# A row softmax on one core: sixteen equal loads become ten loads of 3, 5, 8 and 16 rows per partition, with a store plan of their own

## The chip, the cores and the metric

One core of a Trainium2 chip. The time is device microseconds of one launch. The kernel before was run four times: 162.23 to 162.66 us, median 162.4 us. The profile shown here is of an execution of 162.53 us.

## The reference

```python
def reference(x):                       # x: 16 x 1024 x 512, float32
    x_max = np.max(x, axis=-1, keepdims=True)
    exp_x = np.exp(x - x_max)
    return (exp_x / np.sum(exp_x, axis=-1, keepdims=True)).astype(np.float32)
```

It is a softmax over the last axis. There are 16384 rows of 512 values. Input and output are 33.55 MB each, and nothing but these crosses between HBM and the core's SBUF.

## The kernel before

The 16384 rows are cut into 16 chunks (`CHUNKS`), each of 1024 rows: 8 rows for every one of the 128 partitions. In HBM the 8 rows of one partition lie side by side, so that a load or a store moves 128 runs of 16 KB, 2 MB together. SBUF holds 12 such chunks (`SLOTS`), 96 rows or 192 KB of every partition.

Each chunk passes through five functions.

- `load` (L68) is one DMA on SP's queue, from HBM into one of the 12 buffers.
- `rowmax` (L73) is one VectorE reduction over the 8 rows, which gives 128x8 negated maxima (`shift`).
- `exps` (L79) is 8 ScalarE activations, one for each row: the exponential with the maximum as its bias, written in place, with the sum of the row beside it (`sums`).
- `scale` (L91, L93) is one VectorE reciprocal of the 8 sums and 8 VectorE multiplications in place, one for each row.
- `store` (L100) is one DMA on ScalarE's own queue, from SBUF to HBM. A wait of this DMA stands in ScalarE's order of work, so that the activations of later chunks are held up behind it.

The order on each engine is that in which the program writes it (`manual_schedule`): load, rowmax and exps of chunk k, then scale and store of chunk k-1. VectorE therefore does the maximum of chunk k while the exponentials of chunk k-1 are made, and then scales chunk k-1. Loads 12 to 15 use the buffers of chunks 0 to 3 and wait for the stores of those to land. The DMAs share eight completion semaphores in turn, and a DMA waits for the one that had its semaphore before: load 6, for example, waits until load 0 has landed. Some waits of loads and of stores come from that alone.

`first_load_at_the_head` puts the first load ahead of the barrier with which the program opens.

Of the kernel before, what the change touches and what calls it, by code (L numbers as in the profile page):

```python
# [1 line left out]

# [4 lines left out]

F32 = mybir.dt.float32
EXP = mybir.ActivationFunctionType.Exp
AX = mybir.AxisListType.X  # L10


CHUNKS = [8] * 16

SLOTS = {8: 12}


def first_load_at_the_head(nc):

    main, body = nc.main_func.blocks[0], nc.main_func.blocks[1]  # L20
    dmas = [i for i in body.instructions if type(i).__name__ == "InstDMACopy"]
    load = dmas[0]
    assert load.engine == mybir.EngineType.SP
    body.instructions.remove(load)
    barrier = next(
        n
        for n, i in enumerate(main.instructions)
        if i.engine == mybir.EngineType.SP and type(i).__name__ == "InstDrain"
    )
    main.instructions.insert(barrier, load)  # L30


@with_exitstack
def kernel(
    ctx: ExitStack,
    tc: tile.TileContext,
    x: bass.AP,
    out: bass.AP,
):
    nc = tc.nc  # L40
    nc.at_finalize(first_load_at_the_head)
    P = nc.NUM_PARTITIONS

    x_flat = x.flatten_outer_dims()
    out_flat = out.flatten_outer_dims()
    n, d = x_flat.shape
    assert n == P * sum(CHUNKS)


    src, dst, at = [], [], 0  # L50
    for R in CHUNKS:
        for flat, views in ((x_flat, src), (out_flat, dst)):
            part = flat[at : at + P * R, :]
            views.append(part.rearrange("(p r) d -> p r d", r=R))
        at += P * R

    data = ctx.enter_context(tc.tile_pool(name="data", bufs=1))
    stats = ctx.enter_context(tc.tile_pool(name="stats", bufs=4))

    K = len(CHUNKS)  # L60
    tiles = [None] * K
    shift = [None] * K
    sums = [None] * K

    def load(k):
        R = CHUNKS[k]
        tiles[k] = data.tile([P, R, d], F32, name=f"x{R}", tag=f"x{R}", bufs=SLOTS[R])
        nc.sync.dma_start(out=tiles[k], in_=src[k])  # L68

    def rowmax(k):  # L70
        R = CHUNKS[k]
        shift[k] = stats.tile([P, R], F32, name=f"shift{R}", tag=f"shift{R}")
        nc.vector.reduce_max(out=shift[k], in_=tiles[k], axis=AX, negate=True)  # L73

    def exps(k):
        R = CHUNKS[k]
        sums[k] = stats.tile([P, R], F32, name=f"sums{R}", tag=f"sums{R}")
        for r in range(R):
            nc.scalar.activation(  # L79
                out=tiles[k][:, r, :],  # L80
                in_=tiles[k][:, r, :],
                func=EXP,
                bias=shift[k][:, r : r + 1],
                scale=1.0,
                accum_out=sums[k][:, r : r + 1],
            )

    def scale(k):
        R = CHUNKS[k]
        recip = stats.tile([P, R], F32, name=f"recip{R}", tag=f"recip{R}")  # L90
        nc.vector.reciprocal(out=recip, in_=sums[k])  # L91
        for r in range(R):
            nc.vector.tensor_scalar_mul(  # L93
                out=tiles[k][:, r, :],
                in0=tiles[k][:, r, :],
                scalar1=recip[:, r : r + 1],
            )

    def store(k):
        nc.scalar.dma_start(out=dst[k], in_=tiles[k])  # L100

    with tc.manual_schedule():
        for k in range(K):
            load(k)
            rowmax(k)
            exps(k)
            if k >= 1:
                scale(k - 1)
                store(k - 1)
        scale(K - 1)  # L110
        store(K - 1)


# [1 line left out]
_INS = ['x']  # L115
_OUTS = [((16, 1024, 512), 'float32')]


# [23 lines left out]
```

## Time and profile before

| | |
|---|---|
| time, median of 4 runs | 162.4 us |
| the profiled execution | 162.53 us, its span 160.7 us |
| VectorE (DVE) busy | 123.8 us, 77% of the span |
| ScalarE (ACT) busy | 93.2 us, 58% |
| bytes moved by DMA | 67.14 MB, mean 418 GB/s |
| first load | issued at 0.00 us, landed by 7.85 us |
| last store | issued at 149.08 us |

The span runs from the first instruction of the program to its last; 1.8 us of the execution's time lie around it. "GB/s" in the slices counts every byte once, whether it is read from HBM or written to it. In the queue table, q1 is SP's queue (the loads), q10 is ScalarE's (the stores).

### The profile page before, as it was taken

To read this page: it belongs to the slowest core of one execution; us is meant where nothing else is said; L and a number is where in the kernel's file an instruction comes from. 1 tells how busy PE (TensorE), PEld (TensorE's weight loads), DVE (VectorE), ACT (ScalarE), POOL (GpSimd) and SP (SyncE) were. 2 spreads that over 40 slices of the span, in tenths; PEclk is the share of its full clock that TensorE was granted. 3 is DMA by queue.
4 is the path that set the end of the run, shared out by engine and by line. 5 is a ranking of instruction groups with operands and counts; after the bars stand their busy time and mean duration, and the time that the engine had idled before them with its cause. 6 is when DMAs were issued, how large, how long until landed. Compare 5 with 4: busy or idle time off the path is not lost.

```text
span 160.7 us, 527 instructions
## 1 busy us (share of the span) xinstructions
DVE 123.8 (77%) x160; ACT 93.2 (58%) x257; POOL 0.2 (0%) x4
## 2 busy tenths in 40 slices
DVE  0098799999999999985960089999999999967000
ACT  0029985868677685076002987859595959592000
POOL 0000000000000000000000000000000000000000
DMA  7999999999999999999999999999999999999994
GB/s 241 412 448 424 428 453 338 424 430 428 424 444 436 418 424 436 440 428 424 444 428 428 428 424 448 424 426 428 424 453 424 428 424 432 444 424 428 440 428 175
DMA packets 4611, 67.14 MB, mean 418 GB/s; under 512 B 512, under 2 KB 512, under 8 KB 512
## 3 DMA queue, kind: packets, MB, share of 16 engines
q1 hardware_dynamic: 2304, 33.56, 49.9%
q10 hardware_dynamic: 2304, 33.56, 48.8%
q14 instruction: 3, 0.02, 0.0%
HBM read 33.55 MB, written 33.55 MB: 417 GB/s over the span
## 4 chain that ended last, share of the span: by engine, by line
DMA 52%; DVE 31%; ACT 7%; SPq 1%; issue 1%; ACTq 0%; DVEq 0%
DMA x<-in_x_dram 52%; DVE shift L73 16%; DVE x L93 14%; ACT x L79 7%; SPq L68 1%; DVE recip L91 1%; ACTq L100 0%; DVEq L137 0%; ACTq L79 0%
## 5 line engine op out<-in xcount | busy, mean ns | idle before, releaser
L79 ACT ACTIVATE x<-x,shift 128x512 f32<-128x512 f32 x128 | 90.5, 708 | 44.5 <-DVE shift L73 21.1
L73 DVE TENSOR_REDUCE shift<-x 128x8 f32<-128x4096 f32 x16 | 70.6, 4414 | 9.1 <-DMA x<-in_x_dram 9.1
L93 DVE TENSOR_SCALAR x<-x,recip 128x512 f32<-128x512 f32 x128 | 52.1, 481 | 0.6
L79 ACT ACTIVATION_READ_ACCUMULATOR x<-x,shift 128x1 f32 x128 | 23.9, 187 | 0.0
L91 DVE RECIPROCAL recip<-sums 128x8 f32<-128x8 f32 x16 | 3.1, 195 | 15.6 <-ACT x L79 15.6
L79 ACT ACT_TABLE_LOAD x1 | 1.3, 1283 | 7.9 <-DMA x<-in_x_dram 7.9
L126 POOL MEMSET const-uint8-127<- 128x1 uint8 x1 | 0.1, 103 | 0.0
L126 POOL MEMSET const-bfloat16-1.0<- 128x1 bf16 x1 | 0.1, 102 | 0.0
L126 POOL MEMSET const-float32-0.0<- 128x1 f32 x1 | 0.1, 99 | 0.2 <-issue 0.2
L126 POOL MEMSET const-float32-1.0<- 128x1 f32 x1 | 0.1, 99 | 0.0
## 6 DMA issues: line engine op xcount, KB each, us to landing
x<-in_x_dram SPq DMA_DIRECT2D x16, 2048.0 KB, 42.5
out_dram<-x ACTq DMA_DIRECT2D x16, 2048.0 KB, 17.7
```

The source lines that it names most:

```text
L68: nc.sync.dma_start(out=tiles[k], in_=src[k])
L73: nc.vector.reduce_max(out=shift[k], in_=tiles[k], axis=AX, negate=True)
L79: nc.scalar.activation(out=tiles[k][:, r, :], in_=tiles[k][:, r, :], func=EXP, bias=shift[k][:, r : r + 1], scale=1.0, accum_out=sums[k][: ...
L91: nc.vector.reciprocal(out=recip, in_=sums[k])
L93: nc.vector.tensor_scalar_mul(out=tiles[k][:, r, :], in0=tiles[k][:, r, :], scalar1=recip[:, r : r + 1],)
L126: nc = _bacc.Bacc("TRN2", target_bir_lowering=False, num_devices=1)
```

## The change

The 12 buffers become one array of 96 rows per partition, `held`, and every chunk has a fixed place in it (`CHUNKS` holds pairs of row count and first row). There are ten chunks, of 3, 5, 8 and seven times 16 rows. Eight loads (96 rows) are issued ahead of everything; load 8 goes where chunks 0, 1 and 2 were and is issued once the last of their stores is written, and load 9 goes where chunk 3 was.

A chunk of 16 rows is worked on in two groups of 8 rows, so that `rowmax`, `exps` and `scale` keep their size but for the first two chunks (3 and 5 rows). `FINISH_BEFORE` has VectorE scale chunks 0, 1 and 2 before it begins on the next chunk, instead of after that chunk's maximum. From chunk 3 on the order is as before.

A store covers 3, 5 and 8 rows for the first three chunks, 8 rows for each half of chunks 3, 4 and 5 (`STORE_ROWS`), and 16 rows for chunks 6 to 9. `ON_ACT` is empty, so all loads stay on SP's queue, and `AT_HEAD` puts one load ahead of the barrier, as before. A partition's rows within a chunk still lie side by side in HBM, so a load of 16 rows moves 128 runs of 32 KB; a store of half a chunk moves 128 runs of 16 KB that stand 32 KB apart.

```diff
@@ -10,24 +10,43 @@
 AX = mybir.AxisListType.X
 
 
-CHUNKS = [8] * 16
+CHUNKS = [
+    (3, 0), (5, 3), (8, 8), (16, 16), (16, 32), (16, 48), (16, 64), (16, 80), (16, 0), (16, 16),
+]
+SBUF_ROWS = 96
 
-SLOTS = {8: 12}
+EARLY = 8
+AFTER_STORE = {2: [8], 3: [9]}
+
+GROUP = 8
+
+FINISH_BEFORE = (1, 2, 3)
+
+STORE_ROWS = {3: 8, 4: 8, 5: 8}
+
+ON_ACT = ()
+
+AT_HEAD = {mybir.EngineType.SP: 1}
 
 
-def first_load_at_the_head(nc):
+
+def loads_at_the_head(nc):
 
     main, body = nc.main_func.blocks[0], nc.main_func.blocks[1]
-    dmas = [i for i in body.instructions if type(i).__name__ == "InstDMACopy"]
-    load = dmas[0]
-    assert load.engine == mybir.EngineType.SP
-    body.instructions.remove(load)
-    barrier = next(
-        n
-        for n, i in enumerate(main.instructions)
-        if i.engine == mybir.EngineType.SP and type(i).__name__ == "InstDrain"
-    )
-    main.instructions.insert(barrier, load)
+    for engine, count in AT_HEAD.items():
+        loads = [
+            i
+            for i in body.instructions
+            if i.engine == engine and type(i).__name__ == "InstDMACopy"
+        ][:count]
+        barrier = next(
+            n
+            for n, i in enumerate(main.instructions)
+            if i.engine == engine and type(i).__name__ == "InstDrain"
+        )
+        for load in loads:
+            body.instructions.remove(load)
+        main.instructions[barrier:barrier] = loads
 
 
 @with_exitstack
@@ -38,17 +57,17 @@
     out: bass.AP,
 ):
     nc = tc.nc
-    nc.at_finalize(first_load_at_the_head)
+    nc.at_finalize(loads_at_the_head)
     P = nc.NUM_PARTITIONS
 
     x_flat = x.flatten_outer_dims()
     out_flat = out.flatten_outer_dims()
     n, d = x_flat.shape
-    assert n == P * sum(CHUNKS)
+    assert n == P * sum(R for R, _ in CHUNKS)
 
 
     src, dst, at = [], [], 0
-    for R in CHUNKS:
+    for R, _ in CHUNKS:
         for flat, views in ((x_flat, src), (out_flat, dst)):
             part = flat[at : at + P * R, :]
             views.append(part.rearrange("(p r) d -> p r d", r=R))
@@ -56,59 +75,78 @@
 
     data = ctx.enter_context(tc.tile_pool(name="data", bufs=1))
     stats = ctx.enter_context(tc.tile_pool(name="stats", bufs=4))
+    held = data.tile([P, SBUF_ROWS, d], F32, name="held")
+    place = [held[:, s : s + R, :] for R, s in CHUNKS]
 
-    K = len(CHUNKS)
-    tiles = [None] * K
-    shift = [None] * K
-    sums = [None] * K
+
+    groups = []
+    for k, (R, _) in enumerate(CHUNKS):
+        m = max(1, round(R / GROUP))
+        cuts = [R * i // m for i in range(m + 1)]
+        since = 0
+        for a, b in zip(cuts, cuts[1:]):
+            ends = b == R or b - since >= STORE_ROWS.get(k, R)
+            groups.append((k, a, b, since if ends else None))
+            since = b if ends else since
+    shift = [None] * len(groups)
+    sums = [None] * len(groups)
 
     def load(k):
-        R = CHUNKS[k]
-        tiles[k] = data.tile([P, R, d], F32, name=f"x{R}", tag=f"x{R}", bufs=SLOTS[R])
-        nc.sync.dma_start(out=tiles[k], in_=src[k])
+        queue = nc.scalar if k in ON_ACT else nc.sync
+        queue.dma_start(out=place[k], in_=src[k])
 
-    def rowmax(k):
-        R = CHUNKS[k]
-        shift[k] = stats.tile([P, R], F32, name=f"shift{R}", tag=f"shift{R}")
-        nc.vector.reduce_max(out=shift[k], in_=tiles[k], axis=AX, negate=True)
+    def rowmax(g):
+        k, a, b, _ = groups[g]
+        shift[g] = stats.tile([P, b - a], F32, name="shift", tag="shift")
+        nc.vector.reduce_max(
+            out=shift[g], in_=place[k][:, a:b, :], axis=AX, negate=True
+        )
 
-    def exps(k):
-        R = CHUNKS[k]
-        sums[k] = stats.tile([P, R], F32, name=f"sums{R}", tag=f"sums{R}")
-        for r in range(R):
+    def exps(g):
+        k, a, b, _ = groups[g]
+        sums[g] = stats.tile([P, b - a], F32, name="sums", tag="sums")
+        for r in range(a, b):
             nc.scalar.activation(
-                out=tiles[k][:, r, :],
-                in_=tiles[k][:, r, :],
+                out=place[k][:, r, :],
+                in_=place[k][:, r, :],
                 func=EXP,
-                bias=shift[k][:, r : r + 1],
+                bias=shift[g][:, r - a : r - a + 1],
                 scale=1.0,
-                accum_out=sums[k][:, r : r + 1],
+                accum_out=sums[g][:, r - a : r - a + 1],
             )
 
-    def scale(k):
-        R = CHUNKS[k]
-        recip = stats.tile([P, R], F32, name=f"recip{R}", tag=f"recip{R}")
-        nc.vector.reciprocal(out=recip, in_=sums[k])
-        for r in range(R):
+    def scale(g):
+        k, a, b, since = groups[g]
+        recip = stats.tile([P, b - a], F32, name="recip", tag="recip")
+        nc.vector.reciprocal(out=recip, in_=sums[g])
+        for r in range(a, b):
             nc.vector.tensor_scalar_mul(
-                out=tiles[k][:, r, :],
-                in0=tiles[k][:, r, :],
-                scalar1=recip[:, r : r + 1],
+                out=place[k][:, r, :],
+                in0=place[k][:, r, :],
+                scalar1=recip[:, r - a : r - a + 1],
             )
-
-    def store(k):
-        nc.scalar.dma_start(out=dst[k], in_=tiles[k])
+        if since is not None:
+            nc.scalar.dma_start(
+                out=dst[k][:, since:b, :], in_=place[k][:, since:b, :]
+            )
+        if b == CHUNKS[k][0]:
+            for later in AFTER_STORE.get(k, ()):
+                load(later)
 
     with tc.manual_schedule():
-        for k in range(K):
+        for k in range(EARLY):
             load(k)
-            rowmax(k)
-            exps(k)
-            if k >= 1:
-                scale(k - 1)
-                store(k - 1)
-        scale(K - 1)
-        store(K - 1)
+        waiting = None
+        for g, (k, a, _, _) in enumerate(groups):
+            if waiting is not None and a == 0 and k in FINISH_BEFORE:
+                scale(waiting)
+                waiting = None
+            rowmax(g)
+            exps(g)
+            if waiting is not None:
+                scale(waiting)
+            waiting = g
+        scale(waiting)
 
 
 # ---- launch: one core; inputs and outputs as the reference has them ----
```

## The prediction

> **What bounds the kernel now.** I read the page's slices first, then the DMA queues, a table of stretches, and last the chain and the timeline for the order at both ends.
>
> ```profile
> DVE  0098799999999999985960089999999999967000
> ACT  0029985868677685076002987859595959592000
> DMA  7999999999999999999999999999999999999994
> GB/s 241 412 448 424 428 453 338 424 430 428 424 444 436 418 424 436 440 428 424 444 428 428 428 424 448 424 426 428 424 453 424 428 424 432 444 424 428 440 428 175
> DMA packets 4611, 67.14 MB, mean 418 GB/s; under 512 B 512, under 2 KB 512, under 8 KB 512
> ```
>
> The DMA row is full from the second slice to the last but one. VectorE and ScalarE have holes, in the middle too, and the DMA row stays at 9 across them. DMA is the bound, and the only question about the engines is whether they keep its two queues filled.
>
> ```profile
> 0.00:4.00 4.00, 0.00 (x0) 0.00 (x0) 0.20 (x4) 1.00 0.78 238
> 4.00:24.00 20.00, 14.72 (x12) 12.67 (x33) 0.00 (x0) 1.00 1.01 430
> 24.00:28.00 4.00, 3.96 (x7) 2.06 (x6) 0.00 (x0) 1.00 0.99 348
> 28.00:84.00 56.00, 52.01 (x65) 32.44 (x92) 0.00 (x0) 1.00 1.01 431
> 84.00:92.00 8.00, 0.00 (x0) 4.58 (x13) 0.00 (x0) 1.00 1.02 436
> 92.00:128.00 36.00, 34.63 (x50) 27.86 (x79) 0.00 (x0) 1.00 1.00 430
> 128.00:156.00 28.00, 18.47 (x29) 13.55 (x38) 0.00 (x0) 1.00 1.01 431
> 156.00:160.70 4.70, 0.00 (x0) 0.00 (x0) 0.00 (x0) 1.00 0.52 223
> ```
>
> The last column is GB/s. It is 430 with loads alone (4 to 24 us), with both queues (28 to 84) and with stores alone (128 to 156): one ceiling, whatever the mix. 67.11 MB at 430 GB/s are 156.1 us. Against 430, the first stretch loses 4.00 x (1 - 238/430) = 1.8 us, that at 24 us loses 0.76 us (the first store's packets begin at 25.5 us, and load packets around them are slow), and the end loses 2.3 us. 156.1 + 4.9 = 161.0, the span of 160.7 within the rounding. So only four things can move the time: the cost of a packet, the start, the dip, and a queue that runs dry.
>
> ```profile
> 93.43 3.26 DVE x L93 x8
> 96.69 4.33 DVE shift L73
> 101.02 0.12 DVE recip L91
> 101.14 0.02 issue
> 101.17 3.26 DVE x L93 x8
> ```
>
> These lines of the chain give VectorE's pace: 8 rows every 101.17 - 93.43 = 7.74 us, 272 GB/s of stores, well under 430.
>
> Three lines of the timeline give the landing of the first two loads (VectorE waits for both) and the issue of the last store:
>
> ```profile
> 7.85 4.42 DVE L73 TENSOR_REDUCE shift<-x 128x8 f32<-128x4096 f32 x1 [7.85 <-DMA x<-in_x_dram]
> 12.71 4.42 DVE L73 TENSOR_REDUCE shift<-x 128x8 f32<-128x4096 f32 x1 [0.44 <-DMA x<-in_x_dram]
> 149.08 0.34 ACTq L100 DMA_DIRECT2D out_dram<-x  x1
> ```
>
> **Packets.** The trace records each DMA packet. Nearly all runs of 16 KB took 611 ns each, the three packets of 8 KB that fetch code in the span took 309 ns, the 4-byte ones (a DMA's completion) 9 ns. What a packet costs beyond its bytes is then 2 x 309 - 611 = 7 ns. The bounds: 3 ns by the shortest 8 KB packets on record (307 ns), 9 ns by the whole of a 4-byte packet. I take 7, from the rows nearest in size and time. Before, each of the 16 engines moves 32 DMAs x 8 = 256 data packets. After, 10 loads and 13 stores make 184. 72 x 7 = 0.50 us less; nine completions fewer are 9 x 9 ns = 0.08 us. Together -0.58 us (-0.30 to -0.73).
>
> No row shows a packet over 16 KB. If a 32 KB run goes as two of 16 KB, there are 272 packets and 16 more than before, and this term is +0.1 us.
>
> **The start.** Loads land 4.87 us apart while alone (7.85 and 12.71 in the timeline), so 3 rows need 1.83 us. The first packet of load 0 comes 1.0 us after its issue at 0.00. Load 1 is issued at 0.78 and may begin at 1.8; load 0 keeps the engines to 2.8 or later. That hides load 1's latency, with 1.0 us to spare. The slow first packets (some 0.8 of the 1.8 us) stay; a smaller first packet could save half of it or repeat it once: -0.4 to +0.8, taken as 0, since the loss is spread over the first 1.5 us and not per byte.
>
> The Trainium skill, "DMA: Bandwidth & Descriptors", section Bandwidth, speaks against a 3-row load: it wants 1 MiB or more per DMA, and this is 0.75 MiB. Its table has 78% of peak at 1 MB, which would make of the 3- and 5-row transfers some 0.5 us each, an estimate by that page, and the sum about +1.5 us. Here transfers queue behind one another, and the row of 4 to 24 us holds four load borders at 430.
>
> **Who gets the engines.** In 28 to 84 us the packet records have 734 of loads and 737 of stores, one of each in turn on an engine. I take it that turns go by packet. Then a 32 KB load packet (1.21 us) against a 16 KB store packet (0.61) gives loads two thirds: 1.09 rows per us, against 0.55 for stores (1.64 rows per us is all). By bytes it would be 0.82 each.
>
> The same page, section Queues, rings and completion order, says that an engine goes round the queues packet by packet. By that rule loads get two thirds and the sum below stands; were the turns by bytes, the second rival would be the sum.
>
> **VectorE's new order.** Priced by the rows: maximum 4.33 us for 8 rows (1.65 for 3, 2.76 for 5), exponentials 5.75 for 8 (2.1 and 3.6), reciprocal and scale 3.4 to 3.5 (1.5, 2.3). Load 0 lands at 7.85 - 3.0 = 4.8. Chunk 0 is done and stored at 10.1, chunk 1 at 18.7, chunk 2 at 32.3 (each alone, VectorE idle under the exponentials: 2.1 + 3.6 + 5.8 us, behind DMA that is full). Then maxima of both halves of chunk 3, and its stores at 46.0 and 53.8; from there 7.73 per group: 61.5, 69.2, 76.9, 84.7, chunk 6 at 100.1, 7 at 115.6, 8 at 131.0. The last group's maximum ends at 135.4, its exponentials at 141.2, its scale and store 9 come at 144.7.
>
> Is data there? Chunks 3 to 9 are wanted at 32, 46, 61, 77, 92, 108, 123. Store 0 starts some 4 us after issue (25.5 against 21.61 before) and takes turns with 32 KB packets: 8 x (0.24 + 1.21) = 11.6 us; store 1 12.8, store 2 14.6, so the store queue stays busy from 14. Loads have then 53 rows in by 39, and land 64 by 51, 80 by 65, 96 by 80, 112 by 95, 128 by 109. Every wait is met 10 us or more early. Load 8 waits for store 2 (about 55) and load 9 for chunk 3's second half (about 85); the load queue has work to 79 and, with load 8, to 94. No DMA gap.
>
> Stores that wait in ScalarE's queue would hold exponentials. By the semaphores those are: chunk 5's first store for load 6 (65 against 76.9), chunk 6's for chunk 3's second store (85 against 100), chunk 8's for chunk 4's first (98 against 131). All free in time. The wait of before at 86.98, 10 us of VectorE, goes with it, but DMA was full under it, so it is worth nothing.
>
> **The end.** Loads done by 108, the rest is stores at 430 GB/s. Store 9 is 4.19 MB, 9.75 us (before, 2.10 MB issued at 149.08). DMA would end its data at about 158.5, so what stands ahead of store 9 lasts to 148.7. It is issued at 144.7: 4.0 us of cover, of which up to 3.9 (issue to first packet, the longest seen) is used. Cost 0, and past that 1 us per us of delay.
>
> **Sum.** -0.58 + 0 + 0 (dip once, as before) = 162.53 - 0.58 = 161.95 for the profiled execution, which stands 0.13 above the median; 161.8 by the median.
>
> **Rivals.**
> 1. Forecast, queues full, 0.70: 161.8, own range 161.2 to 162.4.
> 2. 32 KB runs are cut, or turns go by bytes: loads get 0.82 rows per us, 16 rows in 19.6 us against VectorE's 15.5. Chunk 6 comes 3 us late, and chunks 7 to 9 4.1 each, 15.2 in all. Store 9 is issued at 159.9; with 1.0 + 9.75 + 1.1 to its end and 1.8 around the span, 173.6 us. For it: no packet over 16 KB is on record. Against: strict turns of whole packets. It decides once chunk 9 lands after 127 or so. 0.12.
> 3. Store 9 comes too late: a VectorE or ScalarE delay of 1 to 3 us beyond its cover gives 162.8 to 164.8. For: the cover is 4.0 us against a possible 3.9. Against: in the last 30 us of before, a store issued behind others shows no gap (431). Decides from an issue after 144.8 to 147, by the true lag. 0.10.
> 4. The dip of 0.76 us comes with each of the small early stores: two or three more, 163.3 to 164.1. Against: the second start of the store queue before, at 90.4 us after 6 us without a packet, lies in a row of 436. 0.08.
>
> **How the numbers follow.** About 0.2% (0.32 us) is what a measurement tells from no change. In case 1 the packet term alone spans -0.30 to -0.73, and start and dip add some 0.3 either way: of its 0.70, 0.52 faster, 0.15 same, 0.03 slower. Cases 2, 3 and most of 4 are slower, 0.28, with 0.02 of 4 same. Faster 0.52, same 0.17, slower 0.31. The range of 161.2 to 165.0 takes in cases 3 and 4 and leaves out case 2 and the tails of case 1.
>
> **What would show it.** Right: packets 4096 to 2944 of data, the longest at twice 611 ns; 430 GB/s in all slices but the ends; loads finished near 109; store 9 issued at 145. Wrong: a slice under 400 in the middle, VectorE idle on loads after 50 us, or DMA below 9 tenths before the last slice.

## The result, and the profile after

The changed kernel takes 161.62 us in the median of 38 runs (161.48 to 162.78), the kernel before 162.40 us in 56 runs (162.18 to 162.86). The ratio is 0.9964, 95% interval 0.9956 to 0.9972: 0.36% faster. The forecast was 161.8 us. Ten of the 38 runs of the changed kernel lie above 162.0 us, so the two ranges overlap. The profiled execution took 161.54 us, with a span of 159.8.

The page of the changed kernel, its slices and its queue table:

```profile
DVE  0473780699699999999999999999999999853000
ACT  0626209306994959595959586777768685940000
DMA  7998999999999999999999999999999999999993
GB/s 224 432 500 371 408 465 455 393 409 461 410 445 427 476 410 412 435 402 496 418 414 435 402 501 410 412 443 394 451 435 476 402 418 476 418 418 451 427 410 164
DMA packets 3315, 67.13 MB, mean 420 GB/s; under 512 B 368, under 2 KB 368, under 8 KB 624
...
q1 hardware_dynamic: 1440, 33.56, 49.5%
q10 hardware_dynamic: 1872, 33.56, 48.9%
```

The DMA row is as full as it was. The GB/s of single slices scatter more, since a packet counts where it begins and may now be 32 KB; the slices of 371, 393 and 394, under the 400 that the forecast had named as a sign of being wrong, stand beside slices of 443 to 500. VectorE's hole near 85 to 93 us is gone and new ones stand in the first 30 us; neither moved the DMA row. 3315 packets, less 368 completions of 4 bytes and 3 code fetches, are 2944 of data (before, 4096).

The stretches of the changed kernel; the last column is GB/s:

```profile
0.00:4.00 4.00, 0.00 (x0) 0.00 (x0) 0.20 (x4) 1.00 0.74 224
4.00:12.00 8.00, 4.72 (x6) 3.51 (x7) 0.00 (x0) 1.00 1.10 466
12.00:16.00 4.00, 1.22 (x1) 2.75 (x8) 0.00 (x0) 1.00 0.93 387
16.00:112.00 96.00, 87.40 (x108) 64.02 (x180) 0.00 (x0) 1.00 1.00 431
112.00:156.00 44.00, 30.58 (x49) 22.99 (x64) 0.00 (x0) 1.00 1.01 433
156.00:159.80 3.80, 0.00 (x0) 0.00 (x0) 0.00 (x0) 1.00 0.34 147
```

The ceiling is the same 430 to 433. The stretch at 24 to 28 us that stood at 348 before has no successor as deep: store 0 begins at 14.1 us, and 12 to 16 stands at 387 beside 466 for the 8 us ahead of it (packets that begin early in one count for the other).

Of VectorE's own order, the chain and the timeline of the changed kernel show the steady groups and the last store:

```profile
92.87 4.33 DVE shift L101
97.20 0.12 DVE recip L121
97.32 0.02 issue
97.34 3.26 DVE held L123 x8
100.60 4.33 DVE shift L101
```

```profile
145.26 0.34 ACTq L129 DMA_DIRECT2D out_dram<-held  x1
```

The pace is the 7.73 us of before, and store 9 goes out at 145.26 us (forecast 144.7). The forecast is 0.4 us early at the first store and 0.5 to 0.6 from the second on: VectorE gets load 0 at 4.96 us, not 4.8, and the first maximum and exponentials took some 0.25 us longer than reckoned.

From the packet records of the two profiled executions, per DMA engine. "By size" is the number of packets times the usual recorded duration of each size; "slow" is what packets took beyond that. Landings and intervals are those of the completions, as the mean over the 16 engines.

| | before | after |
|---|---|---|
| data packets, completions | 256, 32 | 184, 23 |
| usual duration of 6, 10, 16, 32 KB | -, -, 611, - ns | 234, 385, 611, 1213 ns |
| by size | 156.70 us | 155.96 us |
| slow, first 4 us | 0.91 us | 0.83 us |
| slow, where the store queue starts | 0.79 us | 0.17 us |
| first 16 rows landed | 11.87 us (2 loads) | 11.88 us (3 loads) |
| from one store to the next, stores alone | 4.865 us for 8 rows | 4.865 us for 8 rows, 9.686 us for 16 |
| last data packet ends: mean of the engines, last engine | 158.70, 159.60 us | 157.69, 158.54 us |

By the records the packets' own time fell by 0.74 us and the slow packets by some 0.6, more together than the 1.01 us that the engines gained in the mean (the last engine, which sets the time, gained 1.06 us and the span 1.0 us). The records are no price list, because those of neighbouring packets overlap: the records of an 8-row store add up to 8 x 611 + 9 = 4897 ns, and the next store's completion comes after 4865. The intervals give the price. Two stores of 8 rows take 2 x 4.865 = 9.730 us, one of 16 rows 9.686: eight packets and one completion fewer are worth 0.044 us, some 5 ns apiece. With both queues busy it is the same: 24 rows took 1.5 x 9.727 = 14.59 us before and 14.546 after. The change saves 72 packets and 9 completions, nine times that, 0.40 us. The first 16 rows land at the same time, so the other 0.6 us were gained behind them, and the only place where the records show it is the start of the store queue.

### The profile page after: what moved, and what is told of

Read it like the earlier page. It is cut to its first block, busy times and chain, and to the rows that moved or that the text cites. A ratio compares the mean times of both kernels' runs of the same rounds, so it can differ in the third digit from the quotient of the medians.

```text
span 159.8 us, 521 instructions
## 1 busy us (share of the span) xinstructions
DVE 123.9 (78%) x162; ACT 93.3 (58%) x257; POOL 0.2 (0%) x4
## 2 busy tenths in 40 slices
DMA packets 3315, 67.13 MB, mean 420 GB/s; under 512 B 368, under 2 KB 368, under 8 KB 624
## 4 chain that ended last, share of the span: by engine, by line
DVE 70%; ACT 14%; DMA 3%; issue 3%; DVEq 0%; ACTq 0%
DVE shift L101 38%; DVE held L123 30%; ACT held L109 14%; DMA held<-in_x_dram 3%; DVE recip L121 2%; DVEq L175 0%; ACTq L109 0%
## 5 line engine op out<-in xcount | busy, mean ns | idle before, releaser
L109 ACT ACTIVATE held<-held,shift 128x512 f32<-128x512 f32 x128 | 90.5, 708 | 43.4 <-DVE shift L101 33.2
L101 DVE TENSOR_REDUCE shift<-held 128x8 f32<-128x4096 f32 (+2 forms) x17 | 70.7, 4161 | 5.0 <-DMA held<-in_x_dram 5.0
L123 DVE TENSOR_SCALAR held<-held,recip 128x512 f32<-128x512 f32 x128 | 52.2, 482 | 0.6
L109 ACT ACTIVATION_READ_ACCUMULATOR held<-held,shift 128x1 f32 x128 | 23.8, 186 | 0.0
L121 DVE RECIPROCAL recip<-sums 128x8 f32<-128x8 f32 (+2 forms) x17 | 3.3, 194 | 15.8 <-ACT held L109 15.8
```

Source lines behind the costliest of these rows:

```text
L101: nc.vector.reduce_max(out=shift[g], in_=place[k][:, a:b, :], axis=AX, negate=True)
L109: nc.scalar.activation(out=place[k][:, r, :], in_=place[k][:, r, :], func=EXP, bias=shift[g][:, r - a : r - a + 1], scale=1.0, accum_out=s ...
L121: nc.vector.reciprocal(out=recip, in_=sums[g])
L123: nc.vector.tensor_scalar_mul(out=place[k][:, r, :], in0=place[k][:, r, :], scalar1=recip[:, r - a : r - a + 1],)
```

## The experiments

Six undo or move one part of the change, two delay VectorE at the end, one goes on with larger runs, and one repeats the changed kernel. The kernel before had 162.4 us beside each of them.

**Packet sizes of the two queues turned round.** In the changed kernel, a load of 16 rows is cut in two, and the stores of chunks 3 to 5 are whole:

```diff
-STORE_ROWS = {3: 8, 4: 8, 5: 8}
+STORE_ROWS = {}
 ...
-        queue.dma_start(out=place[k], in_=src[k])
+        R = CHUNKS[k][0]
+        for a in range(0, R, 8):
+            b = min(a + 8, R)
+            queue.dma_start(out=place[k][:, a:b, :], in_=src[k][:, a:b, :])
```

> Loads of 16 rows are issued as two of 8 (16 KB packets), and all stores from chunk 3 on take 16 rows (32 KB packets): the sizes are turned round. Theory (turns by packet): from chunk 3's store on, loads get a third, 0.55 rows per us, against 1.03 that VectorE uses: VectorE waits on loads from about 100 us on, the last load lands at 135 to 145 us instead of 109, store 9 comes 10 to 20 us late and the time is 170 to 180 us. Rival (turns by bytes, or the share does not matter): loads keep at least half, the last load lands by 130 us, and only packets count: 56 - 24 more per engine, +0.3 us, 162 us.

Measured: 172.73 us, ratio 1.063 (1.061 to 1.066). The last load lands at 144.5 us. VectorE's waits and the stretches of this kernel:

```profile
DVE shift L104 <- DMA held<-in_x_dram: 17.9, 6, 6.7
```

```profile
136.00:140.00 4.00, 3.96 (x3) 0.32 (x1) 0.00 (x0) 1.00 0.77 332
140.00:144.00 4.00, 3.00 (x8) 4.00 (x13) 0.00 (x0) 1.00 0.43 184
144.00:152.00 8.00, 7.08 (x9) 4.03 (x12) 0.00 (x0) 1.00 0.94 401
152.00:156.00 4.00, 1.50 (x5) 3.15 (x10) 0.00 (x0) 1.00 0.31 131
156.00:160.00 4.00, 2.67 (x7) 0.00 (x0) 0.00 (x0) 1.00 0.30 131
```

VectorE waited on loads six times, and the DMA engines then stood idle for more than half of 140 to 144 and of 152 to 160 us, because the last stores were not made yet. The packet records give the reason. Where both queues are busy:

| | load packets, store packets | loads, stores in rows per us |
|---|---|---|
| changed kernel, 56 to 108 us (32 and 16 KB) | 452, 459 | 1.09, 0.55 |
| whole stores, 62 to 118 us (32 and 32 KB) | 369, 368 | 0.82, 0.82 |
| this kernel, 60 to 100 us (16 and 32 KB) | 374, 333 | 0.58, 1.04 |

The turns go by packet: nearly equal counts in each row, so that the shares of the two queues stand as their packet sizes do. (The last row has fewer store packets, since stores were not always there to take their turn.)

**Whole stores alone.** The first of the two edits above.

> All stores from chunk 3 on take 16 rows (chunks 3, 4 and 5 were stored in halves). Theory (a packet costs 9 ns beyond its bytes, as 2 x 611 - 1213 ns in the changed kernel shows, and the two queues take turns by packet): 24 packets and 3 completions fewer per engine, -0.24 us, 161.4 us. Load and store packets are then of one size, so loads fall from 0.67 of the traffic to half once chunk 3 is stored (54 us on): the last load lands near 122 us instead of 109. That is just before the 123.8 us at which chunk 9 is wanted, so no loss. Rival (turns by bytes): the share of loads stays as it is and the last load lands at 109 us. Rival (the cover is thinner than I think): VectorE waits on loads from 85 us on, and store 9 comes late, 162.5 us or more.

Measured: 161.96 us (161.70 to 163.39), ratio 0.9994 (0.997 to 1.002), unclear. The last load's completions run from 122.2 to 126.4 us, so the share fell to half as the packet theory has it, but VectorE waited for chunk 9 (3.4 us), store 9 was issued at 148.28, and its first packet began at 149.13, when most engines had been idle, some since 147.6. The saving (0.24 us in the working, 0.13 by the intervals) was spent there. The run went the way of the rival on the cover, below its price. The profiled execution was the longest one, 163.39 us; what it shows of the engines stands further down.

**Half loads alone.** The second of the two edits.

> Loads of 16 rows go as two of 8 (16 KB packets); the stores stay as in the changed kernel. Theory (9 ns a packet, turns by packet): 56 data packets and 7 completions more per engine, +0.57 us, 162.2 us; turns become one to one with the stores of 8 rows, so the last load lands near 130 us instead of 109, against 131.5 at which its half is wanted: just no loss, store 9 at 145 to 147 us. On top of it, if the slow load packets at the start of the store queue go with 16 KB load packets (0.79 us per engine in the kernel before and 0.78 with half loads and 16-row stores, 0.2 to 0.4 with 32 KB load packets), +0.5 us, 162.7 us. Rival (packets cost nothing, the gain of the change lies elsewhere): 161.6 us.

Measured: 168.16 us, ratio 1.035 (1.033 to 1.037). My working missed by 5.5 us. The last load landed at 139.7 us, not 130: loads got 0.80 to 0.82 rows per us from 59 to 107 us, as reckoned, but only 0.60 from 108 to 138, against 1.04 for the stores. Chunks 6 to 9 are still stored in 16 rows, 32 KB packets, and beside those 16 KB load packets get little more than a third; the working had taken one to one to the end. VectorE waited 3.33 and 1.85 us for the last two loads. A second thing was not in the working either: a store of which VectorE had made the data at 76.8 us waited until 84.50, just after a load's last completion at 84.0. In the trace that store has the completion semaphore of the load that ended at 84.0, and the exponentials behind it on ScalarE were held:

```profile
84.50 0.34 ACTq L132 DMA_DIRECT2D out_dram<-held  x1
84.97 0.72 ACT L112 ACTIVATE held<-held,shift 128x512 f32<-128x512 f32 x1 [5.70 <-DVE held L126]
90.74 0.20 DVE L124 RECIPROCAL recip<-sums 128x8 f32<-128x8 f32 x1 [1.85 <-ACT held L112]
```

VectorE waited 1.85 us for them here and 1.89 once more. These waits and those for loads add up to 8.9 us, about the 8.7 us by which the last store came later than in the changed kernel (153.97 against 145.26). So the run doesn't price packets alone, nor load packets alone: a part of the loss goes with the order of the semaphores. It does show that slow packets come back (0.84 us per engine at 12 to 24 us, against 0.17 in the changed kernel, with the same first stores of 3 and 5 rows).

**Stores of 8 rows to the end.**

```diff
-STORE_ROWS = {3: 8, 4: 8, 5: 8}
+STORE_ROWS = {k: 8 for k in range(3, 10)}
```

> All stores take 8 rows, those at the end too. Theory: 32 packets and 4 completions more per engine, 32 x 9 + 4 x 9 ns = +0.32 us, 161.95 us; nothing else moves, since these stores run after the last load. Rival (the size of the last store sets the end): the last store is 2 MB instead of 4 MB, so its 4.9 us less of transfer after the last scale would show as a gain, 161.6 us or less.

Measured: 161.83 us (161.80 to 161.91), 0.21 above the changed kernel's median. By size the packets take 156.28 us per engine, 0.32 more than in the changed kernel by the records; by the intervals (four stores of 16 rows become eight of 8) it is 4 x 0.044 = 0.18 us. The 0.21 measured (0.25 against the repeat of the changed kernel) is too near to both to tell them apart; the intervals do. The size of the last store sets nothing: half of it was no gain.

**One first chunk of 8 rows.**

```diff
-    (3, 0), (5, 3), (8, 8), (16, 16), (16, 32), (16, 48), (16, 64), (16, 80), (16, 0), (16, 16),
+    (8, 0), (8, 8), (16, 16), (16, 32), (16, 48), (16, 64), (16, 80), (16, 0), (16, 16),
```

(with the numbers of the chunks in the other lists moved down by one)

> The first two chunks (3 and 5 rows) become one of 8 rows. Theory of packets: 16 packets and 2 completions fewer per engine, -0.16 us, 161.45 us. VectorE begins at 7.9 instead of 5.0 us and store 9 is issued about 2.2 us later, 147.5 us, against 148.8 us at which the store ahead of it ends: free if a store behind another needs under 1.3 us from issue to first packet. Rival (the slow load packets when the store queue starts, 0.79 us per engine before the change and 0.17 us after it, come with the size of the first store's packets): they come back with 16 KB packets, +0.6 us, 162.1 us. Rival (a store needs 3.9 us from issue to first packet even behind another): +2.6 us, 164.0 us.

Measured: 161.96 us (161.90 to 162.06), 0.34 above the changed kernel though it has 16 packets fewer. Its last store, and the stretches around it:

```profile
147.71 0.34 ACTq L129 DMA_DIRECT2D out_dram<-held  x1
```

```profile
144.00:146.00 2.00, 1.79 (x5) 0.14 (x2) 0.00 (x0) 1.00 1.10 475
146.00:148.00 2.00, 1.67 (x5) 0.00 (x0) 0.00 (x0) 1.00 0.76 328
148.00:150.00 2.00, 0.00 (x0) 0.00 (x0) 0.00 (x0) 1.00 1.16 492
150.00:152.00 2.00, 0.00 (x0) 0.00 (x0) 0.00 (x0) 1.00 0.69 295
```

The packet records put the first packet of this store at 148.55 us, 0.84 after its issue. Most engines had ended the store ahead between 147.9 and 148.5, and the mean engine passed some 0.5 us without a packet before this store. The slow packets at the start of the store queue were 0.34 us, against the 0.79 of the first rival, which is near in time alone. So the 3- and 5-row chunks are worth something: they put store 9 out 2.5 us earlier.

**Store 9 late by a known amount.** Ahead of the last group's maximum, over 4 rows in one kernel and over 8 in the other:

```diff
+            if g == len(groups) - 1:
+                spare = stats.tile([P, 8], F32, name="spare", tag="spare")
+                nc.vector.reduce_max(
+                    out=spare, in_=place[k][:, a : a + 8, :], axis=AX, negate=True
+                )
             rowmax(g)
```

> One spare maximum over 4 rows stands before the last group's maximum on VectorE, its result unused: store 9 is issued 2.2 us later, at 147.0 to 147.5 us. The engines end the store ahead between 147.6 and 148.9 us. In two runs a store behind others had its first packet 0.84 us after its issue. Theory (0.84 us): it starts at 147.9 to 148.3, the engines lose 0.2 to 0.7 us each but the slowest, which sets the end, loses nothing: 161.6 to 162.0 us. Rival (3.9 us from issue to first packet, the longest seen, also behind another store): 151 us, +2.5 us, 164 us.

> The same with a spare maximum over 8 rows: store 9 is issued 4.4 us later, at 149.2 to 149.6 us. Theory (0.84 us from issue to first packet): it starts at 150.2, the engines end together 9.7 us later, at 160.0, so the span is 161.1 and the time 162.9 us. Rival (3.9 us): 166 us. Rival (the cover is over 4 us): 161.6 us.

Measured: 161.96 us with 4 rows (161.57 to 162.84, so not told apart from the changed kernel), store 9 issued at 146.91 us in the profile. With 8 rows 162.81 us (162.77 to 163.01). Of the kernel with 8 rows:

```profile
149.08 0.34 ACTq L129 DMA_DIRECT2D out_dram<-held  x1
```

```profile
146.00:148.00 2.00, 2.00 (x6) 0.00 (x0) 0.00 (x0) 1.00 0.76 328
148.00:150.00 2.00, 1.05 (x3) 0.00 (x0) 0.00 (x0) 1.00 0.38 164
150.00:152.00 2.00, 0.00 (x0) 0.00 (x0) 0.00 (x0) 1.00 0.85 360
```

All 16 engines had ended the store ahead, at 147.7 to 148.9, when this one was issued, and its first packet came at 149.93. The time lies 0.09 us from what 0.84 us from issue to first packet gives. The other lag (3.9 us: 164 and 166) is excluded by both runs.

**One chunk of 13 rows for those of 5 and 8**, in groups of 6 and 7 rows, with the next maximum ahead of its scale:

```diff
-    (3, 0), (5, 3), (8, 8), (16, 16), ...
+    (3, 0), (13, 3), (16, 16), ...
-FINISH_BEFORE = (1, 2, 3)
+FINISH_BEFORE = (1,)
```

> The chunks of 5 and 8 rows become one of 13, worked on in groups of 6 and 7 rows, and VectorE no longer finishes it before the next chunk's maximum. Theory of packets: 16 packets and 2 completions fewer per engine, -0.16 us, 161.45 us. VectorE gets through the first chunks about 7 us earlier, so store 9 is issued near 138 us, which is worth nothing by itself. Loads are wanted 7 us earlier too (chunk 9 at 117 us) and the last lands at 108. Rival (VectorE's order is part of the bound): 7 us earlier would show as a gain of over 0.5 us. Rival (a load of 13 rows starves VectorE at the start and the cover of the end is spent): 162 us or more.

Measured: 162.50 us (161.85 to 163.08), ratio to before 0.9997 (0.998 to 1.001). VectorE's order did what was reckoned, store 9 was issued at 138.36 us, 6.9 earlier, and that was no gain: VectorE is not the bound. The 16 packets fewer were no gain either. In the profile, the load packets at 32 to 36 us, where store 1 starts a queue that had been empty since 25 us, were slow by 0.54 us per engine:

```profile
28.00:32.00 4.00, 3.96 (x10) 3.12 (x9) 0.00 (x0) 1.00 1.10 475
32.00:36.00 4.00, 4.00 (x1) 2.63 (x8) 0.00 (x0) 1.00 1.01 377
```

**Runs of 64 KB.** Chunks of 3, 5, 8, 16 and three times 32 rows:

```diff
-    (3, 0), (5, 3), (8, 8), (16, 16), (16, 32), (16, 48), (16, 64), (16, 80), (16, 0), (16, 16),
+    (3, 0), (5, 3), (8, 8), (16, 16), (32, 32), (32, 64), (32, 0),
-        ends = b == R or b - since >= STORE_ROWS.get(k, R)
+        ends = b in {4: (16, 32), 5: (16, 32), 6: (16, 24, 32)}.get(k, (R,))
```

> After the chunks of 3, 5, 8 and 16 rows come three of 32 rows (loads of 64 KB runs, work still in groups of 8), stored in 16s and the last in 16, 8 and 8. Theory (9 ns a packet whatever its size, turns by packet): 40 data packets and 5 completions fewer per engine, -0.40 us, 161.2 us; a 64 KB packet takes 2 x 1213 - 9 = 2417 ns. VectorE gets its chunk of 32 rows about 3 us late near 47 us, and the last load waits for the store of the fourth chunk, so it lands at 110 to 113 us against 108 to 111 wanted; the 8 rows at the end leave store cover for that. Rival (a run of 64 KB is cut in pieces of 32 KB or less): packets stay at 32 KB, turns as in the changed kernel, 161.6 us. Rival (the store of a small packet waits out long load packets, the last load comes 10 us late or more): 165 us.

Measured: 164.11 us (163.66 to 165.20), ratio 1.012 (1.009 to 1.015). A 64 KB run goes as one packet, of 2418 ns (2417 reckoned). By the records the packets took 155.58 us per engine, 0.38 less than in the changed kernel. But the last load landed at 114.8 to 116.8 us and VectorE waited for it; store issues fell behind and the engines paused at 138 to 142 us:

```profile
DVE shift L101 <- DMA held<-in_x_dram: 13.7, 3, 7.8
```

```profile
138.00:140.00 2.00, 2.00 (x6) 2.00 (x6) 0.00 (x0) 1.00 0.46 197
140.00:142.00 2.00, 2.00 (x3) 2.00 (x7) 0.00 (x0) 1.00 0.61 262
```

The last load was issued only at 81.80 us, once the store of the fourth chunk had landed (81.35). From 49 to 70 us, 64 KB load packets beside 16 KB store packets, loads got 1.21 rows per us and stores 0.35. That is the way of the last rival, at about half its delay. There were, too, 0.90 us of slow packets at 84 to 88 us, where the last load came in beside stores after 16 us without a load packet.

**The changed kernel again.**

> The changed kernel itself, beside the one with 64 KB runs. Its times so far lie at 161.5 to 161.7 us in most executions and at 162.4 to 162.8 in some. Theory (engines that are always busy never even out, so that one that loses about 1 us at the start ends as much later): 161.6 us, some executions 1 us above; in the profile, the 16 completions of the second load and those of the last store are spread alike, by about 1 us where the time is 161.6 and by 2 where it is 162.6. Rival (store 9 late in some executions): the spread of the last completions is small where the time is 162.6, and the engines pause before it.

Measured: 161.58 us (161.56 to 162.45, seven runs), ratio 0.9959 (0.9943 to 0.9975). The spread of 16 completions, first to last engine, from the packet records:

```
                       time of the execution   second load   last store
before                       162.53 us           0.65 us      1.44 us
changed kernel               161.54              0.94         1.22
changed kernel again         161.61              0.91         1.26
stores of 8 rows             161.80              1.35         1.21
spare maximum, 8 rows        162.85              0.84         0.17
whole stores                 163.39              1.99         1.36
```

The engines are uneven from the first two loads on, by 0.6 to 2 us, and are still 1.2 to 1.4 us apart at the end where they do not pause. A pause of all of them before the last stores evens them out: with the spare maximum over 8 rows the spread is 0.17 us, and its ten times lie within 0.24 us; in the three other kernels whose engines ran dry near the end (half loads, sizes turned round, 64 KB runs) it is 0.15 to 0.18. In the profiled execution of the kernel with whole stores one engine was 0.92 us behind the other fifteen by the second load and ended 1.2 us after the next one. That speaks for uneven engines as the source of the executions near 162.6 us of the changed kernel, but no profile of the changed kernel was such an execution, so it is not shown for it.

## Why the prediction was right, step by step

- **The bound.** Right. DMA stayed full at 430 to 433 GB/s; 6.9 us of VectorE earlier was worth nothing.
- **Packets (-0.58, between -0.30 and -0.73).** Right in mechanism, too large in size. I subtracted recorded durations (7 ns; those of the changed kernel would give 2 x 611 - 1213 = 9 ns, which the texts of the experiments use). But the records overlap, and on the clock a packet or a completion costs some 5 ns: 9 x 0.044 = -0.40 us, within the range.
- **The start (0).** Right for this pair of profiles: 0.83 us of slow packets against 0.91, no gap between loads 0 and 1, and the first 16 rows landed at 11.88 against 11.87 us. In the nine other profiles with a first load of 3 rows the slow packets were 0.24 to 0.67 us and the 16 rows landed at 11.46 to 11.84 in the mean, so some of the half that I had thought possible does come in some executions; the last engine had them at 12.0 to 12.5 us in eight of the nine (13.2 in one), against 12.3 before.
- **The dip (taken as unchanged, 0.76).** Mis-sized: by the records 0.17 us in place of 0.79. It goes with the load packets. With 32 KB loads it was 0.17 in the changed kernel and 0.2 to 0.4 in seven others at the first start; with 16 KB loads 0.79 before and some 0.8 in both kernels with half loads. Why large load packets lose less at that moment stays open, and the kernels with 26 KB stores or 64 KB loads had larger dips later. The kernel with the sizes turned round had some later too (0.56 us at 124 to 128).
- **The sum.** -0.40 for the packets and -0.6 for the dip make -1.0, which is what the engines gained in the mean (1.01) and the span (1.0); the forecast had -0.58 and 0. The packet term was too large by 0.18 us and the dip, the larger part of the gain, was put at nothing. That 161.8 came within 0.2 us of the median is in part luck: the two errors have opposite signs, and between the medians the gain is 0.78 us, less than the 0.99 between the two profiled executions.
- **Who gets the engines.** Right to the figure: 1.09 and 0.55 rows per us, and the last load landed at 108.3 to 109.5 us (forecast 109). The Trainium skill, "DMA: Bandwidth & Descriptors", section Queues, rings and completion order, says turns go packet by packet; 452 load and 459 store packets in 52 us agree.
- **The page's wish for 1 MiB per DMA** (section Bandwidth) would have put the sum at some +1.5 us because of the small first transfers, by the estimate in the forecast. Its table is of DMAs issued from GpSimd; these are issued from SP and ScalarE. Here 6 KB packets took 234 ns, 26.3 bytes per ns against 26.8 at 16 KB, and three loads brought the first 16 rows as early as two did (11.88 and 11.87 us). For loads that follow one another on a queue, the measurement decides against the rule.
- **VectorE's order.** Right within 0.6 us from the first store (10.52 against 10.1) to the last (145.26 against 144.7).
- **The end.** The cost of 0 was right, the margin was not. I had 4.0 us of cover, up to 3.9 of it used. The engines end the store ahead from 147.6 us on, and a store with no loads beside it needs 0.84 us, so 1.5 us are left. The 3.9 was measured beside loads, of which none are left at the end. With store 9 at 147.71 engines already paused; at 149.08 it cost 1.2 us of the time.
- **Rivals.** The second (loads at half the traffic, 173.6 us) did not happen here. Kernels that force such shares show the price: 162.0 us with half the traffic from 57 us on (whole stores), 168.2 with half and later a third (half loads, with the semaphore's part in it), 172.7 with a third. The third is the kernel with the spare maximum over 8 rows. The fourth, slow packets at more than one start, did not happen here, but did in the kernels with a 13-row chunk, with 64 KB runs and with the sizes turned round.

## What to carry to other kernels

Where DMA is full from end to end, count packets, and price them by the interval from one completion to the next, not by the difference of recorded durations: here some 5 ns each on the clock where the records say 9. The larger gain, 0.6 us, lay at the moment at which a second queue starts beside a busy one, which the forecast had taken as fixed. Packet size also sets which queue gets the engines, since two queues take turns packet by packet; a size that saves packets on one side can starve the other, as stores of 16 rows beside loads of 8 did by 11 us. Give the last store cover by what stands ahead of it on the engines, and price it with the lag measured in the same condition, here that of stores with no loads beside them, not the longest one on the page.

## What the runs showed of the hardware that I had not expected

- Packets of 6, 10, 16, 32 and 64 KB took 234, 385, 611, 1213 and 2418 ns in the records: one line, with 8 to 9 ns at its start. On the clock the price of a packet is less, some 5 ns (9.730 against 9.686 us for 16 rows).
- A store that finds engines free of loads has its first packet 0.84 to 0.85 us after its issue, whether the engines have run dry (149.08 to 149.93 with the spare maximum over 8 rows) or still end another store (147.71 to 148.55 with one first chunk of 8). A store issued into an empty store queue beside loads took 3.4 to 4.1 us (10.52 to 14.11 in the changed kernel: 3.6; 21.61 to 25.50 before: 3.9; 86.98 to 90.42 before, the second start: 3.4). What makes the difference was not tested apart.
- The 16 engines are 0.6 to 2 us apart at the second load and, where they do not pause, 1.2 to 1.4 us at the end; a pause of all of them brought them within 0.2 us. The last of them sets the time, not their mean.
